# One norm's sums taken by TensorE, layer 0's set-up put behind the first feed-forward, and half a product put between two products on the same PSUM banks

## The chip, the cores and the metric

One core of a Trainium2 chip runs the whole program. The metric is the device time of one execution in microseconds (us); the time before is the median of three executions. Engines are named as in the profile: PE (TensorE), DVE (VectorE), ACT (ScalarE), POOL (GpSimd), SP (SyncE), and a "q" behind a name means its queue of DMA issues. All data are fp32.

## What is computed

Two decoder layers over 512 tokens of width 1024. Each layer is a feed-forward at half weight, a mixer, and a second feed-forward at half weight. The mixer of layer 0 is a hybrid (Mamba-2 heads beside mLSTM heads), that of layer 1 is sparse attention with a top-k choice of keys. Every one of the six stages starts from an RMS norm.

```python
def rms_norm(x, g):
    xf = x.astype(jnp.float32)
    y = xf * lax.rsqrt(jnp.mean(xf * xf, axis=-1, keepdims=True) + EPS) * g.astype(jnp.float32)
    return y.astype(x.dtype)

def swiglu(h, w_gate, w_up, w_down):          # D_MODEL 1024, D_FF 2816
    return (jax.nn.silu(h @ w_gate) * (h @ w_up)) @ w_down
...
x = x + 0.5 * swiglu(rms_norm(x, ffn_norm[l, 0]), ...)
x = x + mixer(rms_norm(x, mix_norm[l]), ...)
x = x + 0.5 * swiglu(rms_norm(x, ffn_norm[l, 1]), ...)
```

## The kernel before

**Stages and layout.** The stages run in the order ffn00, mix0, ffn01, ffn10, mix1, ffn11. The state x lies transposed in SBUF, as eight tiles of 128 features by 512 tokens (k = 0 to 7). An fp32 product is made as three matmuls of split operands, high by high, high by low and low by high (`mm3`, L263 to L265), so each operand exists as a pair of forms: ACT rounds the high part (L436) and DVE subtracts it to get the low part (L438).

**A feed-forward.** The 2816 hidden features are 11 units of 256 columns in three groups of 4, 4 and 3 units (`GROUPS`). When a group's hidden tiles are there, `down` multiplies them by the group's rows of the down-projection, for n = 0 and n = 1 (512 output features each). `down` calls `seven`, a product of two by two blocks in seven products instead of eight. The products accumulate in pairs of PSUM banks: A (tile `pA`), and D or B (tiles `pD` and `pB`, of one tag). A product is two halves (s = 0, 1), each of 12 matmuls of 256 columns in a group of four units and 9 in the group of three. Between products that go on in the same banks, what stands there is taken out first: `keep` copies it to SBUF on ACT (L581), and `c11`, `c22`, `c12` and `c21` add it to what was kept on DVE (L431 `ft<-pA,ft`) and then to x (L779). With n = 0 (`late=True`) the order of the seven products is A(A11), B(A12), D(S1), A(S2), A(S3), D(S4), A(A22); the two halves of A's S2 are kept by two ACT copies of 256 columns, after which S3 starts on the same banks. With n = 1 the order is A, D, A, B, A, D, A. There are 12 calls with n = 0: three groups in each of four feed-forwards.

**Forms of the weights.** `block` loads a piece of weights over SP's queue into one of 4 raw buffers, and `made` writes its forms into one of 5 form buffers. For S4 and A12 the form is "summed": ACT writes the negated high part (L463), a DMA on POOL's queue adds the raw weights onto it (L464), and ACT writes the high part (L465).

**What sets the order.** In the feed-forwards the steps are recorded in a `Plan` with a cost in us each; a list scheduler orders them and they are issued in that order on every engine, PE's in the order of the code. ffn00 is one plan, ffn01 with ffn10 the second, ffn11 the third. The code of the mixers and of the set-up is put in order by the framework's own scheduler. Each engine executes its instructions in order.

**The norm between stages.** As the last call of `down` finishes x, `prep_later` runs for each pair of tiles (dp = 0, 1 after n = 0, and 2, 3 after n = 1): ACT writes x times gain (L719), DVE its low part (L722), ACT the square (L732), and POOL adds the squares of k = 1 to 7 one after another onto `ssq` (L431 `ssq<-ssq,sq`, seven adds). `settle` then sums over the features with four matmuls by a column of ones (`pssq`, 8 records on PE, L694 in a plan, L378 otherwise); the last product of n = 1, `c21`, finishes x for dp = 2. The next stage's matmuls on x times gain begin before that; the factor from the norm goes in later (`prow`, then `rrow`). The first stage loads x and makes its norm in `load_x` (`prep`, L348, L366, L367). After the last stage, `store_later` transposes x on PE (`pot`, L803), copies it on ACT (L812) and stores it.

**Layer 0's set-up.** `setup_hybrid` loads four small parameter arrays over ACT's queue (`prow`, L290) and transposes them on PE (`ptpar`, L292); they are first used in mix0. It is called ahead of all stages.

Of the kernel before, what the change touches and what calls it, by code (L numbers as in the profile page):

```python
# [16 lines left out]
P = 128  # L17
# [62 lines left out]
class Plan:  # L80
# [9 lines left out]
    def __init__(self, tc):  # L90
        self.tc, self.steps, self.writer, self.readers, self.last, self.users = tc, [], {}, {}, {}, {}

# [76 lines left out]
    def issue(self):  # L169
        start = self.order()  # L170
        nc = self.tc.nc
        for i in sorted(range(len(start)), key=lambda i: (start[i], i)):
# [3 lines left out]
            for ins in nc.cur_bb.bb.instructions[n:]:  # L176
# [6 lines left out]
                self.last[ins.engine] = ins.name  # L183
        self.__init__(self.tc)
# [19 lines left out]
class Trunk:  # L204
# [146 lines left out]
    def prep(self, which, k):  # L351
# [16 lines left out]
        if k == KC - 2:  # L368
            self.xg, self.pending = [Feat(t) for t in self.xgn], 2
            self.xgk = lambda k: [("xg", which, i, k) for i in range(2)]  # L370

    def rms_col(self, ssq, n):
# [4 lines left out]
        for b in range(NB):  # L377
            nc.tensor.matmul(ps[:, b : b + 1], ssq[:, b * P : (b + 1) * P], self.ones1, start=True, stop=True)  # L378
# [14 lines left out]
    def settle(self):  # L393
# [3 lines left out]
        if self.pending == 2:  # L397
            self.rcol = self.rms_col(self.ssq(), D)
# [157 lines left out]
    def seven(self, raws, xf, late, kept, evac):  # L556
# [10 lines left out]
        def mul(ps, block, form, start, summed=False):  # L567
            j, f = self.made(block, summed)
            ps, psk = ps
            for s in range(2):  # L570
                col = slice(s * P, (s + 1) * P)
                for q in range(nq):
# [3 lines left out]
                    )  # L576

        def keep(to, ps, halves):
            (to, tok), (ps, psk) = to, ps
            for h in ((0, 1), (1, 2)) if halves else ((0, 2),):  # L580
                self.s((h[1] - h[0]) * H, lambda h=h: nc.scalar.activation(  # L581
                    to()[:, h[0] : h[1]], ps()[:, h[0] : h[1], 0:H], AF.Copy), [(*psk, s) for s in range(*h)], tok[h[0] : h[1]])
# [9 lines left out]
        keep(kept[0], A, False)  # L592
        if late:
# [4 lines left out]
            keep(kept[2], D, False)  # L598
            mul(A, less(t2, b22, b11), self.S2, False)
            keep(kept[1], A, True)  # L600
            mul(A, less(b12, b22, b12), self.S3, False)
            c22(A, kept[2])
            mul(D, b22, self.S4, False, True)
            c12(D, kept[1])
        else:
            mul(D, less(b11, b12, b11), self.S1, True)
            keep(kept[2], D, False)
            mul(A, less(t2, b22, b11), self.S2, False)
            keep(kept[1], A, False)
# [73 lines left out]
    def settle_later(self):  # L683

        nc = self.nc
        if self.pending == 2:
# [3 lines left out]
            ssq = self.ssq  # L690

            def sums():
                for b in range(NB):
                    nc.tensor.matmul(ps()[:, b : b + 1], ssq()[:, b * P : (b + 1) * P], self.ones1, start=True, stop=True)  # L694

            self.t(0.6, sums, ["ssq"], ["pssq"])
# [10 lines left out]
    def prep_later(self, which, k):  # L707
# [26 lines left out]
        if k == KC - 2:  # L734
# [893 lines left out]
```

## Time and profile before

| | us |
|---|---|
| median of three executions | 2085.14 (2084.42 to 2085.89) |
| the profiled execution | 2082.31 |
| its span in the trace | 2080.6 |
| PE busy in the span | 2021.5 (97%) |
| DVE busy | 1615.7 (78%) |
| ACT busy | 1148.6 (55%) |

A row of a timeline is: start in us, duration in us, engine, line, operation, output<-input, array and tile sizes, count, and in brackets the idle time of that engine just before it with what ended that idle time. Matmuls are pipelined: one of 256 columns is shown some 0.28 us long, while the next one starts some 0.12 us after it, so costs on PE are read from start to start. Some matmul records can be missing.

### The profile page before, as it was taken

How to read it: one execution, taken by the hardware profiler on the slowest of the kernel's cores; microseconds unless marked ns; L12 is line 12 of the kernel's file. 1: busy time of each engine (PE TensorE's matmuls, PEld its weight loads, DVE VectorE, ACT ScalarE, POOL GpSimd, SP SyncE). 2: the span in 40 equal slices, each digit the busy share in tenths (PEclk: the TensorE clock that was granted, in tenths of full speed). 3: DMA queues.
4: the chain of work that ended last, by engine and by line, in shares of the span. 5: the costliest groups of instructions: out<-in, count | busy, mean ns of one | idle time of the engine just before them, and what ended most of it. 6: DMA issues, size and time to landing. Idle time of an engine off the chain costs nothing.

```text
span 2080.6 us, 34030 instructions
## 1 busy us (share of the span) xinstructions
PE 2021.5 (97%) x13726; PEld 1812.4 (87%) x13726; DVE 1615.7 (78%) x2363; ACT 1148.6 (55%) x1678; POOL 282.0 (14%) x328
## 2 busy tenths in 40 slices
PE   6999999999999999999998999999997999999998
PEld 5999999887788888999998999999864468999998
DVE  5988878786537638989787988878789736988886
ACT  4666656442335435656565666657455624656564
POOL 2000001420001020000002000001215311001000
PEclk8999999999999999999999999999996999999999
DMA  4456565422221222665664456565420012556564
GB/s 134 122 156 170 149 166 131 130 87 71 71 82 61 81 92 81 153 173 149 156 150 114 122 157 169 150 165 134 130 67 11 1 41 71 142 153 165 150 165 110
DMA packets 203174, 248.65 MB, mean 120 GB/s; under 512 B 13452, under 2 KB 181512, under 8 KB 203016
## 3 DMA queue, kind: packets, MB, share of 16 engines
q1 hardware_dynamic: 184720, 185.52, 28.6%
q0 software_dynamic: 17280, 60.83, 15.8%
q8 instruction: 108, 1.77, 0.3%
q14 instruction: 50, 0.41, 0.1%
q10 hardware_dynamic: 1016, 0.13, 0.0%
HBM read 183.53 MB, written 2.10 MB: 89 GB/s over the span
## 4 chain that ended last, share of the span: by engine, by line
PE 92%; DVE 3%; DMA 1%; ACT 1%; issue 1%; POOL 0%; SPq 0%; ACTq 0%; DVEq 0%; POOLq 0%
PE pA L263 10%; PE pA L264 10%; PE pA L265 10%; PE pD L263 5%; PE pD L265 5%; PE pD L264 5%; PE pB L263 3%; PE pB L264 3%; PE pB L265 3%; PE ptok L263 3%; PE ptok L265 3%; PE ptok L264 2%; PE po L265 2%; PE po L263 2%; PE po L264 2%; PE po L1515 2%
## 5 line engine op out<-in xcount | busy, mean ns | idle before, releaser
L438 DVE TENSOR_TENSOR form<-raw,form 128x1024 fp32r<-128x1024 f32 (+1 forms) x332 | 395.7, 1200 | 120.4 <-ACT form L436 119.7
L436 ACT ACTIVATE form<-raw 128x1024 fp32r<-128x1024 f32 (+1 forms) x332 | 339.5, 1027 | 144.0 <-DVE raw L431 100.6
L263 PE MATMUL pA<-xf,form 128*128 128x256 f32 x1152 | 322.4, 280 | 0.0
L264 PE MATMUL pA<-xf,form 128*128 128x256 f32 x1152 | 322.4, 280 | 0.0
L265 PE MATMUL pA<-xf,form 128*128 128x256 f32 x1152 | 321.9, 279 | 0.0
L431 DVE TENSOR_TENSOR raw<-raw 128x1024 f32<-128x1024 f32 (+1 forms) x240 | 283.4, 1185 | 7.6 <-DMA raw<-in_ffn_w_up 3.4
L464 POOL DMA_DIRECT2D form<-raw x120 | 103.4, 861 | 1181.2 <-ACT form L463 1127.0
L263 PEld LDWEIGHTS pA<-xf,form 128*128 128x128 f32 x1152 | 216.8, 188 | 0.1
L264 PEld LDWEIGHTS pA<-xf,form 128*128 128x128 f32 x1152 | 216.3, 188 | 0.2
L265 PEld LDWEIGHTS pA<-xf,form 128*128 128x128 f32 x1152 | 216.4, 188 | 0.0
L263 PE MATMUL pA<-hid,form 128*128 128x256 f32 x704 | 201.0, 286 | 12.0 <-ACT ft L581 11.3
L463 ACT ACTIVATE form<-raw 128x1024 fp32r<-128x1024 f32 (+1 forms) x120 | 123.4, 1028 | 157.5 <-PE pD L265 133.7
L264 PE MATMUL pA<-hid,form 128*128 128x256 f32 x704 | 198.2, 282 | 0.8 <-DVE hid L438 0.8
L265 PE MATMUL pA<-hid,form 128*128 128x256 f32 x704 | 197.5, 281 | 0.0
L265 PE MATMUL pD<-xf,form 128*128 128x256 f32 x576 | 161.5, 280 | 0.0
L264 PE MATMUL pD<-xf,form 128*128 128x256 f32 x576 | 161.3, 280 | 0.0
L263 PE MATMUL pD<-xf,form 128*128 128x256 f32 x576 | 161.3, 280 | 0.0
L232 DVE TENSOR_TENSOR form<-raw,form 128x1024 fp32r<-128x1024 f32 (+2 forms) x85 | 102.3, 1204 | 64.1 <-ACT form L229 61.5
L431 DVE TENSOR_TENSOR ft<-ft 128x256 f32<-128x256 f32 (+2 forms) x288 | 146.9, 540 | 4.1
L229 ACT ACTIVATE form<-raw 128x1024 fp32r<-128x1024 f32 (+2 forms) x85 | 87.0, 1023 | 113.8 <-PE ptok L265 44.2
L263 PEld LDWEIGHTS pA<-hid,form 128*128 128x128 f32 x704 | 132.5, 188 | 17.5 <-ACT ft L581 16.5
L264 PEld LDWEIGHTS pA<-hid,form 128*128 128x128 f32 x704 | 132.4, 188 | 1.8 <-DVE hid L438 1.6
(372 smaller groups left out, 5298.2 us busy)
## 6 DMA issues: line engine op xcount, KB each, us to landing
form<-raw POOLq DMA_DIRECT2D x104, 512.0 KB, 5.6
raw<-in_ffn_w_gate SPq DMA_DIRECT2D x88, 512.0 KB, 4.4
raw<-in_ffn_w_up SPq DMA_DIRECT2D x88, 512.0 KB, 4.1
raw<-in_ffn_w_down SPq DMA_DIRECT2D x64, 512.0 KB, 4.8
raw<-in_hy_w_in SPq DMA_DIRECT2D x44, 512.0 KB, 3.5
raw<-in_ffn_w_down SPq DMA_DIRECT2D x32, 384.0 KB, 3.5
raw<-in_hy_w_out SPq DMA_DIRECT2D x16, 512.0 KB, 3.3
form<-raw POOLq DMA_DIRECT2D x16, 384.0 KB, 4.4
```

The source lines that it names most:

```text
L229: nc.scalar.activation(hi, src, AF.Copy)
L232: nc.vector.tensor_tensor(lo, src, hi.bitcast(F32), op=ALU.subtract)
L263: mm(out, l[0], r[0], start=start, stop=False)
L264: mm(out, l[0], r[1], start=False, stop=False)
L265: mm(out, l[1], r[0], start=False, stop=stop)
L431: (self.p if pool else self.v)(n, lambda: e.tensor_tensor(out(), x(), y(), op=op), reads, writes)
L436: self.s(n, lambda: nc.scalar.activation(hi(), src(), AF.Copy), srck, hik)
L438: n, lambda: nc.vector.tensor_tensor(lo(), src(), hi().bitcast(F32), op=ALU.subtract), srck + hik, lok
L463: self.s(n * w, lambda: nc.scalar.activation(f[:, 1], raw, AF.Copy, scale=-1.0), rawk, lok)
L464: self.plan.add("gpsimd", 0.85, lambda: nc.gpsimd.dma_start(f[:, 1], raw, accum_op=ALU.add), rawk + lok, lok, 5.5)
L1515: nc.tensor.matmul(po[par * 64 : par * 64 + 64], pr[s // 2][:, s % 2, V : V + 64], pT[par], start=(s == 0), stop=(s == b),)
```

## The change

Five edits:
1. In `seven` with `late=True`, A's S2 is kept by one ACT copy of 512 columns, and between S2 and S3 stands the first half (s = 0) of D's S4. Its second half stands where the whole of S4 stood, behind S3. S4's form is made before S3's.
2. In the last call of `down`, the pairs of tiles for n = 1 are prepared (or stored) in the order dp = 3, 2.
3. In `prep_later` the squares of the last pair (dp = 2) are no longer added by POOL. `pssq` takes them as two more operands: twelve matmuls (24 records) in place of four (8), and five POOL adds in place of seven. This is so in the three places where a feed-forward's `prep_later` feeds a norm: from ffn00 to mix0, from ffn01 to ffn10 and from ffn10 to mix1.
4. `setup_hybrid` is called at the start of mix0, behind the last PE instruction of ffn00's plan.
5. `rms_col` and the plan's `sums` share one function.

```diff
-        def mul(ps, block, form, start, summed=False):
-            j, f = self.made(block, summed)
+        def mul(ps, block, form, start, summed=False, f=None, ss=(0, 1)):
+            j, f = made = f or self.made(block, summed)
...
-            for s in range(2):
+            for s in ss:
...
-            keep(kept[1], A, True)
+            keep(kept[1], A)
+            f22 = mul(D, b22, self.S4, False, True, ss=(0,))
             mul(A, less(b12, b22, b12), self.S3, False)
             c22(A, kept[2])
-            mul(D, b22, self.S4, False, True)
+            mul(D, b22, self.S4, False, f=f22, ss=(1,))
             c12(D, kept[1])
...
+    def sums(self, ps, parts):
+
+        for b in range(NB):
+            for i, x in enumerate(parts):
+                self.nc.tensor.matmul(
+                    ps[:, b : b + 1], x[:, b * P : (b + 1) * P], self.ones1, start=i == 0, stop=i == len(parts) - 1
+                )
...
-            self.t(0.6, sums, ["ssq"], ["pssq"])
+            self.t(0.2 + 0.45 * len(ssqs), lambda: self.sums(ps(), [x() for x in ssqs]), self.ssqk, ["pssq"])
...
+            if last:
+                self.ssqs, self.ssqk = self.ssqs + [sq], self.ssqk + sk
+            elif j:
+                ssq = self.ssqs[0]
                 self.vtt(T, ssq, ssq, sq, ALU.add, ["ssq"], ["ssq"] + sk, True)
...
-                for dp in (2 * n, 2 * n + 1):
+                for dp in ((0, 1), (3, 2))[n]:
                     if nxt is None:
                         self.store_later(dp)
                     else:
-                        self.prep_later(nxt, 2 * dp)
+                        self.prep_later(nxt, 2 * dp, dp == 2)
...
-            self.setup_hybrid()
...
                 elif s == "mix0":
+                    with tc.issue_after(self.plan.tail[mybir.EngineType.PE]):
+                        self.setup_hybrid()
                     self.hybrid(nxt)
```

Lines of the change stand one to nine further down: `mm3` is L264 to L266, `keep` L590, the summed form L472 to L474, high parts L445.

**The order on PE in the first call with n = 0.** In the kernel before, these rows stand where S2 ends and S3 begins; a tile's number tells one tile from another of its name.

```order
L265 MATMUL pA_958<-hid_858,form_80 128x256
L263 MATMUL pA_958<-hid_962,form_80 128x256
L264 MATMUL pA_958<-hid_971,form_80 128x256
L265 MATMUL pA_958<-hid_962,form_80 128x256
L263 MATMUL pA_958<-hid_398,form_80 128x256
L264 MATMUL pA_958<-hid_429,form_80 128x256
```

S3's first matmul follows S2's last on the same tile. In the change, the same place reads as follows.

```order
L264 MATMUL pA_948<-hid_952,form_80 128x256
L265 MATMUL pA_948<-hid_961,form_80 128x256
L266 MATMUL pA_948<-hid_952,form_80 128x256
L264 MATMUL pD_1020<-hid_388,form_80 128x256
L265 MATMUL pD_1020<-hid_419,form_80 128x256
L266 MATMUL pD_1020<-hid_388,form_80 128x256
```

Twelve matmuls on pD (three of them shown) now stand between pA's S2 and pA's S3, and twelve fewer stand behind S3.

**The order on ACT ahead of the same place.** In the kernel before, L463 and L465 make S4's summed form and L581 are the keeps.

```order
L643 ACTIVATE ft_782<-pA_736 128x2x256
L436 ACTIVATE hid_962<-ft_782 128x256
L436 ACTIVATE hid_962<-ft_782 128x512
L463 ACTIVATE form_80<-raw_79 128x1024
L436 ACTIVATE hid_858<-ft_567 128x512
L465 ACTIVATE form_80<-raw_79 128x1024
L581 ACTIVATE ft_1047<-pA_958 128x512
```

In the change, L472 and L474 are the summed form and L590 the keep.

```order
L652 ACTIVATE ft_772<-pA_726 128x2x256
L472 ACTIVATE form_80<-raw_79 128x1024
L474 ACTIVATE form_80<-raw_79 128x1024
L445 ACTIVATE hid_952<-ft_772 128x256
L445 ACTIVATE hid_952<-ft_772 128x512
L445 ACTIVATE hid_848<-ft_557 128x512
L590 ACTIVATE ft_1024<-pA_948 128x512
```

The summed form moved ahead of two (its last part: three) instructions that make hidden forms.

**The order on PE at the start of mix0 in the change.** `pgate` are three of mix0's first products, `ptpar` is the set-up's transpose, `pssq` the norm's sums.

```order
L265 MATMUL pgate<-xgn,form 24x512
L266 MATMUL pgate<-xgn,form 24x512
L293 MATMUL ptpar<-raw,prow 128x76
L264 MATMUL pgate<-xgn,form 24x512
L265 MATMUL pgate<-xgn,form 24x512
L266 MATMUL pgate<-xgn,form 24x512
L378 MATMUL pssq<-raw,ssq 128x1
L378 MATMUL pssq<-raw,sq 128x1 x2
```

`ptpar` stood in ffn00's first unit, directly ahead of its `pssq`, and now stands here, 54 matmuls behind the last product of ffn00; three such pairs of `pssq` rows follow the one shown.

## Rows read from the trace of the kernel before

**Rows 1.** The head of the page: span, busy times, and the chain that ended last by engine.

```profile
span 2080.6 us, 34030 instructions
PE 2021.5 (97%) x13726; PEld 1812.4 (87%) x13726; DVE 1615.7 (78%) x2363; ACT 1148.6 (55%) x1678; POOL 282.0 (14%) x328
PE 92%; DVE 3%; DMA 1%; ACT 1%; issue 1%; POOL 0%; SPq 0%; ACTq 0%; DVEq 0%; POOLq 0%
```

**Rows 2.** The waits of PE over the span: us in total, times, longest.

```profile
PE pA L263 <- ACT ft L581: 11.3, 24, 0.5
PE ptpar L292 <- DMA prow<-in_hy_conv_w: 10.4, 1, 10.4
...
PE pssq L694 <- POOL ssq L431: 4.9, 1, 4.9
...
PE ptok L265 <- DVE xgn L722: 2.0, 2, 1.2
...
PE prow L390 <- POOL raw L382: 0.9, 1, 0.9
...
PE pot L803 <- DVE raw L779: 0.7, 2, 0.3
```

**Rows 3.** The timeline of PE where S2 ends and S3 runs, in ffn00's first call with n = 0.

```profile
125.98 0.28 PE L265 MATMUL pA<-hid,form 128*128 128x256 f32 x1
126.74 0.39 PE L263 MATMUL pA<-hid,form 128*128 128x256 f32 x1 [0.47 <-ACT ft L581]
126.96 0.28 PE L264 MATMUL pA<-hid,form 128*128 128x256 f32 x1
...
128.15 0.28 PE L265 MATMUL pA<-hid,form 128*128 128x256 f32 x1
128.90 0.39 PE L263 MATMUL pA<-hid,form 128*128 128x256 f32 x1 [0.47 <-ACT ft L581]
```

**Rows 4.** The timeline of ACT at the same place.

```profile
126.30 0.38 ACT L581 ACTIVATE ft<-pA 128x256 f32<-128x256 f32 x1 [1.16 <-PE pA L265]
...
128.46 0.38 ACT L581 ACTIVATE ft<-pA 128x256 f32<-128x256 f32 x1 [0.83 <-PE pA L265]
```

**Rows 5.** From the views of single lines: durations in ns (least, median, longest) of the instructions that empty pA, and for L464, the DMA that makes the summed form, the time to landing in us.

```profile
L581 ACT ACTIVATE ft<-pA x132: 383/597/603, 80.6 to 2065.1; 128x512 f32<-128x512 f32 x108, 128x256 f32<-128x256 f32 x24
L431 DVE TENSOR_TENSOR ft<-pA,ft x60: 677/692/694, 90.2 to 2069.5; 128x512 f32<-128x512 f32 x60
...
DMA to landing us min/median/max: 3.9/5.5/8.7
```

**Rows 6.** The timeline of POOL: the issue of S4's summed form ahead of the place of rows 3, and the one ahead of the third group's place, where PE's first wait ended at 345.67.

```profile
119.99 0.85 POOL L464 DMA_DIRECT2D form<-raw  x1 [10.12 <-ACT form L463]
...
340.95 0.86 POOL L464 DMA_DIRECT2D form<-raw  x1 [11.05 <-DVE form L438]
```

**Rows 7.** The start of ffn00: PE, then ACT, POOL and the chain of waits (start, us, what).

```profile
21.87 0.40 PE L265 MATMUL pg<-xgn,form 128*128 128x512 f32 x1
32.70 0.36 PE L292 MATMUL ptpar<-raw,prow 76*128 76x76 f32 x1 [10.44 <-DMA prow<-in_hy_conv_w]
32.86 1.81 PE L694 MATMUL pssq<-raw,ssq 128*128 128x1 f32 x8
...
28.06 1.06 ACT L436 ACTIVATE form<-raw 128x1024 fp32r<-128x1024 f32 x1 [6.08 <-DMA raw<-in_ffn_w_gate]
...
30.39 1.26 POOL L367 TENSOR_TENSOR ssq<-ssq,sq 128x512 f32<-128x512 f32 x1 [6.18 <-ACT sq L366]
...
28.07 4.39 DMA prow<-in_hy_conv_w
```

**Rows 8.** From ffn01 to ffn10: PE, then ACT, POOL and DVE.

```profile
1119.36 0.40 PE L265 MATMUL pg<-xgn,form 128*128 128x512 f32 x1
1124.68 1.87 PE L694 MATMUL pssq<-raw,ssq 128*128 128x1 f32 x8 [4.92 <-POOL ssq L431]
1126.41 0.77 PE L263 MATMUL pu<-xgn,form 128*128 128x512 f32 x1
...
1119.89 1.13 ACT L732 ACTIVATE sq<-raw 128x512 f32<-128x512 f32 x2
...
1117.44 7.19 POOL L431 TENSOR_TENSOR ssq<-ssq,sq 128x512 f32<-128x512 f32 x4 [7.32 <-ACT sq L732]
...
1114.31 1.22 DVE L438 TENSOR_TENSOR form<-raw,form 128x1024 fp32r<-128x1024 f32 x1
...
1117.84 2.33 DVE L438 TENSOR_TENSOR form<-raw,form 128x1024 fp32r<-128x1024 f32 x1
1120.09 5.75 DVE L722 SCALAR_TENSOR_TENSOR xgn<-raw,xgn 128x512 fp32r<-128x512 f32 x4
```

**Rows 9.** Windows: for each stretch its length and the busy time (count) of PE, PEld, DVE, ACT and POOL, the granted clock of PE, the share of the DMA engines and GB/s.

```profile
1125.00:1131.00 6.00, 6.00 (x19) 5.04 (x19) 2.05 (x4) 0.00 (x0) 1.03 (x1) 0.50 0.27 87
1470.00:1490.00 20.00, 17.34 (x108) 16.76 (x109) 12.72 (x23) 7.99 (x22) 7.90 (x9) 1.00 0.36 106
1557.00:1600.00 43.00, 29.18 (x100) 18.04 (x99) 42.19 (x124) 21.54 (x56) 28.26 (x24) 0.67 0.04 13
```

**Rows 10.** From ffn00 to mix0: PE's sums, and ACT's last square.

```profile
384.78 0.95 PE L378 MATMUL pssq<-raw,ssq 128*128 128x1 f32 x8
...
379.44 0.61 ACT L732 ACTIVATE sq<-raw 128x512 f32<-128x512 f32 x1
```

More of the change, by code (lines that the diff above doesn't have):

```diff
@@ L182, in issue @@
                     )
-                self.last[ins.engine] = ins.name
-        self.__init__(self.tc)
+                self.last[ins.engine], self.tail[ins.engine] = ins.name, ins
+        self.__init__(self.tc, self.tail)
 class Lazy:
@@ L376, in rms_col @@
         ps = self.aux("pssq", (T,))
-        for b in range(NB):
-            nc.tensor.matmul(ps[:, b : b + 1], ssq[:, b * P : (b + 1) * P], self.ones1, start=True, stop=True)
+        self.sums(ps, ssq)
         ms, rcol = (self.cols[:, self.turn, i] for i in range(2))
@@ L576, in mul, with keep @@
                     )
-        def keep(to, ps, halves):
+            return made
+        def keep(to, ps):
             (to, tok), (ps, psk) = to, ps
-            for h in ((0, 1), (1, 2)) if halves else ((0, 2),):
-                self.s((h[1] - h[0]) * H, lambda h=h: nc.scalar.activation(
-                    to()[:, h[0] : h[1]], ps()[:, h[0] : h[1], 0:H], AF.Copy), [(*psk, s) for s in range(*h)], tok[h[0] : h[1]])
+            self.s(T, lambda: nc.scalar.activation(to(), ps()[:, :, 0:H], AF.Copy), [(*psk, 0), (*psk, 1)], tok)
         def less(o, x, y):
@@ L591, in seven @@
         mul(A, b11, self.A11, True)
-        keep(kept[0], A, False)
+        keep(kept[0], A)
         if late:
@@ L606, in seven @@
             mul(D, less(b11, b12, b11), self.S1, True)
-            keep(kept[2], D, False)
+            keep(kept[2], D)
             mul(A, less(t2, b22, b11), self.S2, False)
-            keep(kept[1], A, False)
+            keep(kept[1], A)
             B = self.pair("pB", "pB")
@@ L689, in settle_later @@
             self.turn, self.rcol = 1 - self.turn, rcol
[L690 to L694, printed above, removed]
-            self.t(0.6, sums, ["ssq"], ["pssq"])
+            ssqs = self.ssqs
+            self.t(0.2 + 0.45 * len(ssqs), lambda: self.sums(ps(), [x() for x in ssqs]), self.ssqk, ["pssq"])
             self.v(4, lambda: nc.vector.tensor_scalar(ms, ps()[:, 0:NB], 1.0 / D, EPS, op0=ALU.mult, op1=ALU.add),
@@ L705, in settle_later, with prep_later @@
         self.pending = max(self.pending - 1, 0)
-    def prep_later(self, which, k):
+    def prep_later(self, which, k, last):
         nc = self.nc
@@ L973, in gate @@
                     yield
-            rc = self.rms_col(ssq, 512)
+            rc = self.rms_col([ssq], 512)
             yield
```

21 lines of the change are left out of this document (11 added, 10 removed).

## The prediction

> **What bounds the kernel now.** I read the head of the page first [rows 1]: PE is busy 97% of the span, and 92% of the chain that ended last is PE. So the change can gain only what PE idles, what PE runs at the lower clock, and PE instructions that go. The waits of PE come next [rows 2]: the two longest entries are 24 waits of 0.5 us on the keep of `pA` (11.3 us) and one of 10.4 us on the set-up's parameters; one of 4.9 us on POOL's sum of squares stands lower. These are the three that the change touches. Then I read each place in the timelines [rows 3, 4, 7, 8, 10]. The sum below is made against the profiled execution: span 2080.6 us, 1.7 us around it, 2082.3 in all. The median of the three timed executions, 2085.1, is 2.8 above it, and I carry the difference over to that.
>
> **Half a product between products.** In before, S2's last matmul starts at 125.98, the keep at 126.30, S3's first matmul at 126.74 and its second at 126.96 [rows 3, 4]. Unhindered, matmuls of 256 columns start 0.12 apart (126.96 to 128.15 in ten steps). So two steps take 0.98 instead of 0.24: one wait costs 0.74, not the 0.47 shown as idle, since the first matmul behind it is slow as well. There are 24 of them [rows 2], two in each of 12 calls: 24 x 0.74 = 17.8 us.
>
> In the change a half of S4 on pD stands in this place. Is it long enough? In the groups of four units it is 12 matmuls, so S3 starts 13 steps after S2's last start, at 1.55 us; in the group of three 9 matmuls, 10 steps, 1.19. The keep needs 0.28 (the last matmul), 0.04 to ACT's start, 0.60 for 512 columns [rows 5], 0.06 back to PE: 0.98. That leaves 0.57 and 0.21. The second half of S4 now covers c22, which is DVE's and takes 0.69 [rows 5]: with the same ends 1.07, leaving 0.48 and 0.12. Both fit if the engine is free. ACT was: it idled 1.16 and 0.83 until PE ended, just before the keeps [rows 4]. For DVE no row shows it, since in before a whole product covered c22. I take all 17.8; the lower bound is nothing (first rival), and more than this isn't there. One keep less per call saves ACT some 0.1, hidden.
>
> **Start.** PE idles from 22.3 to 32.70 for the parameters, then runs `pssq` [rows 7]. Without `ptpar` it waits for the last add on POOL, 30.39 + 1.26 = 31.65. That chain starts from the first weights, which free ACT at 28.06, and none of it moves. So `pssq` starts at 31.7 instead of 32.86: 1.2 gained. Most of the stall stays, and so does the lower clock behind it. Bounds: 0.5 to 1.5.
>
> **ffn01 to ffn10.** Here PE idles 4.92 until POOL has added the last square at 1124.63, though ACT had that square at 1121.02 [rows 8]; then the clock stands at 0.50 for 1125 to 1131 with PE busy throughout [rows 9], work that takes half of those 6 us at full clock. So the stall and its clock cost 4.9 + 3.0 = 7.9. In the change `pssq` waits for ACT's last squares and for the fifth add. `c21` now feeds the last pair, whose two products with the gain and two squares follow on ACT, and five adds end two adds earlier. The adds took 1.8 each beside DVE against 1.26 alone [rows 7, 8], so the fifth ends some 3.6 before 1124.63, at 1121.0, when the squares are ready too. What is left of the wait would be 1121.0 - 1119.8 = 1.3 if nothing else moved; the new order puts ACT's squares ahead of the products with the gain, so I take 0.7, with 0 and 3 as ends. With 0.7 the clock stays: between 1470 and 1490 PE idled 2.7 us in three pieces and kept 1.00 [rows 9]. At full clock eight `pssq` records take 0.95 [rows 10], of which the last one's own length is some 0.17, so 0.11 a record; 16 more cost 1.8. Net: -7.9 + 0.7 + 1.8 = -5.4.
>
> A row shows DVE's form at 1.22 without POOL's adds beside it and 2.33 with them [rows 8]. The Trainium skill, page "SBUF — State Buffer", section "Who interferes with whom", has a rule that fits: a DVE instruction with two SBUF inputs and a GpSimd instruction that reads SBUF share one read port, and the later one is fully blocked until the other ends. The trace agrees in that both get slower. By this rule two adds fewer would give DVE back some 2.2 us in this stretch, and the 0.7 would go to 0; the sum doesn't count on it.
>
> **ffn00 to mix0.** In before no wait shows here; `pssq` runs at 384.78 among full work. The 16 records cost 1.8. `ptpar` costs its 0.2 here. Its four DMAs are issued behind ACT's last squares. These ended at 380.05 in before [rows 10]; the landing took 4.39 after the first issue [rows 7], so 384.4, and `ptpar` stands three matmuls ahead of `pssq`, at about 384. I take no wait; bounds 0 to 3. Net +2.0.
>
> **ffn10 to mix1.** PE waits 2.0 for DVE's products with the gain and 0.9 for `prow` [rows 2]. The change spreads the sums among mix1's first products and puts 21 of these ahead of `prow`, so the 0.9 goes; 1.8 is added; with two adds fewer beside DVE I take half of the 2.0 as gone. Net -0.1, bounds -2 to +2. Behind this the scheduler also reorders DVE's top-k work; DVE is busy 42.2 of 43 us there and PE 29.2 [rows 9], and nothing of that work is added or removed: 0, between -4 and +4.
>
> **Tail.** With dp = 3 stored first, only the last pair's transposes wait for `c21`: of 0.7 of waits [rows 2] I take 0.4.
>
> **The sum.** -1.2 - 17.8 - 5.4 + 2.0 - 0.1 - 0.4 = -22.9. The profiled execution would take 2059.4, the median 2062.2, so 2062.
>
> **Rivals.**
> - *The banks come free late.* With DVE busy 78% [rows 1], `c22` may find it in a form of 1.22, and the keep may find ACT in one of 1.06 [rows 7, 8]. Per call the worst is 1.22 + 1.06 less the spare 0.12 + 0.21 in the 4 calls of three units (1.95) and 0.48 + 0.57 in the other 8 (1.2): 4 x 1.95 + 8 x 1.2 = 17.4, all of the gain. Against it: ACT's idle time ahead of the keeps [rows 4]. Half of it gives 2071.
> - *The sums still wait.* DVE's products with the gain ran to 1125.84 [rows 8], behind POOL's adds. If PE still idles 3 us at ffn10, the clock falls as before: 2.3 + 3.0 lost, with up to 3 at `ptpar`, together 7: 2069.
> - *Slower: S4's summed form comes late.* It is now needed when S2 ends, a product and its waits earlier, and its path runs over ACT, a DMA on POOL's queue and the landing. In before the issue at 119.99 and a median landing of 5.5 [rows 5, 6] give 125.5, 1.2 ahead of 126.74; in the group of three 340.95 + 3.9 (the shortest, for its smaller piece) gives 344.9, 0.8 ahead of 345.67. The gain of 22.9 is eaten at 1.9 a call in 12 calls, so it decides at a landing of some 8.5 us everywhere if the issue stays; the longest seen is 8.7. At 9.5 it is 12 x 2.8 = 33.6 against the 22.9: 2096. Against it: ACT now makes the form's first part two hidden forms earlier.
> - *The change doesn't do what it says.* The 0.74 waits also gave DVE and ACT time to make the next forms. If these bound instead, the stall moves from the keep to `form` or `hid`, and the 17.8 stays: 2080. Against it: no wait of PE for a form shows in [rows 2], and ACT idles at the keeps [rows 4].
>
> On the slower rival's transfer the traces have their row, 5.5 us [rows 5]. The Trainium skill, page "DMA: Bandwidth & Descriptors", section "Anatomy of one DMA — SWDGE (gpsimd) path", gives for such a transfer a fixed 2.0 us and its bytes at 436 GB/s; for 512 KB that would be an estimate of 3.2, by which the rival falls away. The trace's number is longer, and decides.
>
> **Chances.** Forecast 0.70 (its own range 2057 to 2067), banks late 0.11, sums still waiting 0.10, stall moved 0.05, slower 0.04. The range for 8 in 10 reaches from 2055 (two transitions at their better ends, mix1 4 better) to 2072 (either of the first two rivals). About 0.2%, 4.2 us, is what a measurement of this kernel tells from no change. The first three cases are all faster by more; of the stall that moved (-5, near the bound) 0.01 counts as faster and 0.04 as the same: faster 0.92, same 0.04, slower 0.04.
>
> **What would show it.** Right: the row of 24 waits of `pA` on ACT `ft` is gone and no wait on DVE `ft<-pA,ft` takes its place; `ptpar` waits nowhere near ten us; ahead of ffn00's `pssq` PE still idles some 9 us, now for POOL; PE's clock at 1125 to 1131, shifted, is 1.00, and `pssq` has 24 records of 2.7 us in three places. Wrong: waits of PE in each call on `form`, `hid` or DVE `ft`; a clock at 0.50 at the start of ffn10; a wait of `ptpar` in mix0; or a stretch of attention longer by more than 4 us.

## The result, and the profile after

The changed kernel takes 2074.68 us (median of six executions, 2067.87 to 2082.13) against 2085.67 (six, 2084.42 to 2089.04) for the kernel before. The ratio is 0.9946 [0.9923, 0.9969]: faster, by 11 us instead of the 22.9 forecast, and above the range that ended at 2072. The profiled execution took 2076.09; its pair is the 2082.31 from which the sum started.

The head of the page of after, with the chain that ended last by engine, answers to [rows 1].

```profile
span 2074.3 us, 34103 instructions
PE 2029.2 (98%) x13774; PEld 1818.2 (88%) x13774; DVE 1614.9 (78%) x2363; ACT 1147.1 (55%) x1666; POOL 273.4 (13%) x322
...
PE 88%; DVE 5%; DMA 4%; issue 2%; ACT 1%; POOL 0%; SPq 0%; ACTq 0%; POOLq 0%; DVEq 0%
```

PE's busy time has risen by 7.7 us though its waits got fewer: 48 more records, and time at the lower clock, which counts as busy. PE's share of the last chain fell from 92% to 88%, DVE's rose from 3% to 5%. The waits of PE in after answer to [rows 2].

```profile
PE pssq L378 <- POOL ssq L368: 10.2, 1, 10.2
PE pqk L1487 <- DVE st L1492: 6.1, 4, 3.2
...
PE pg L265 <- DVE xgn L726: 1.7, 2, 1.0
PE pA L265 <- DVE hid L447: 1.5, 5, 0.7
...
PE ptok L265 <- DVE form L233: 1.0, 1, 1.0
PE pot L810 <- DVE raw L786: 0.7, 1, 0.7
...
PE pA L264 <- ACT hid L445: 0.6, 1, 0.6
```

The 24 waits on the keep are gone, and no wait for `c22`'s `ft` or for S4's form took their place. The waits of `pA` for hidden forms are 2.1 in all (1.5 on DVE, 0.6 on ACT) where before had 0.8; none of them stands between S2 and S4. `ptpar` waits nowhere. The wait of 4.9 for POOL's sum at ffn10 is gone; two for DVE's `xgn`, 1.7 together, are new. The place of [rows 3], on PE:

```profile
124.78 0.28 PE L266 MATMUL pA<-hid,form 128*128 128x256 f32 x1
124.90 0.28 PE L264 MATMUL pD<-hid,form 128*128 128x256 f32 x1
...
126.20 0.28 PE L266 MATMUL pD<-hid,form 128*128 128x256 f32 x1
126.32 0.28 PE L264 MATMUL pA<-hid,form 128*128 128x256 f32 x1
126.44 0.29 PE L265 MATMUL pA<-hid,form 128*128 128x256 f32 x1
```

And the keep on ACT, which answers to [rows 4]:

```profile
125.10 0.60 ACT L590 ACTIVATE ft<-pA 128x512 f32<-128x512 f32 x1 [0.77 <-PE pA L266]
```

From S2's last start to S3's first are 13 steps of 0.12, 1.54 us. The keep ends at 125.70, 0.62 before S3; the prediction had 1.55 and 0.57. This part came out as worked out.

Where, then, are the other 12 us? The program is cut at attention: from the first transpose of a query on PE (`pqt`, the start of mix1's score work) to the last mixer's end (`prow` of ffn11). The columns of the two views that follow are those of [rows 9]: length, busy times, clock, DMA share, GB/s. First the kernel before:

```profile
1561.51:1743.75 182.24, 170.97 (x649) 102.12 (x649) 118.56 (x310) 85.91 (x196) 64.48 (x80) 0.89 0.09 27
```

Then after:

```profile
1548.52:1741.07 192.55, 179.56 (x648) 104.75 (x649) 120.86 (x308) 86.04 (x196) 65.33 (x80) 0.83 0.08 25
```

The same work takes 10.3 us more, at a granted clock of 0.83 instead of 0.89. Time at the lower of the two levels is 2 x (1 - clock) x length: 40 us before, 65 after (to 2 us, as the clock has two digits). All the rest of the span went from 1898.4 (2080.6 - 182.24) to 1881.8, 16.6 less. By stretch, from the starts of the same PE instructions in both traces:

| stretch | forecast | measured |
|---|---|---|
| start, to ffn00's `prow` | -1.2 | -0.7 |
| ffn00 and mix0 | -2.4 | -2.5 |
| ffn01, to ffn10's `prow` | -9.8 | -7.3 |
| ffn10, to the first `pqt` | -4.5 | -2.5 |
| attention | 0 | +10.3 |
| ffn11 and the tail | -4.8 | -3.6 |

Two questions stand: what each edit gave, and whether attention's 10 us belong to the change.

### The profile page after: what moved, and what is told of

It is laid out like the page before. It is cut to its first block, busy times and chain, and to the rows that moved or that the text cites. A ratio compares the mean times of both kernels' runs of the same rounds, so it can differ in the third digit from the quotient of the medians.

```text
span 2074.3 us, 34103 instructions
## 1 busy us (share of the span) xinstructions
PE 2029.2 (98%) x13774; PEld 1818.2 (88%) x13774; DVE 1614.9 (78%) x2363; ACT 1147.1 (55%) x1666; POOL 273.4 (13%) x322
## 3 DMA queue, kind: packets, MB, share of 16 engines
q8 instruction: 108, 1.77, 0.3%
## 4 chain that ended last, share of the span: by engine, by line
PE 88%; DVE 5%; DMA 4%; issue 2%; ACT 1%; POOL 0%; SPq 0%; ACTq 0%; POOLq 0%; DVEq 0%
PE pA L265 9%; PE pA L264 9%; PE pA L266 9%; PE pD L266 5%; PE pD L265 5%; PE pD L264 5%; PE ptok L266 3%; PE ptok L264 2%; PE ptok L265 2%; PE pB L265 2%; PE pB L264 2%; PE pB L266 2%; PE po L266 2%; PE po L264 2%; PE po L265 2%
## 5 line engine op out<-in xcount | busy, mean ns | idle before, releaser
L445 ACT ACTIVATE form<-raw 128x1024 fp32r<-128x1024 f32 (+1 forms) x332 | 340.0, 1028 | 164.9 <-DVE raw L440 118.3
L264 PE MATMUL pA<-xf,form 128*128 128x256 f32 x1152 | 321.8, 279 | 0.0
L266 PE MATMUL pA<-xf,form 128*128 128x256 f32 x1152 | 321.5, 279 | 0.0
L473 POOL DMA_DIRECT2D form<-raw x120 | 103.6, 863 | 1161.8 <-ACT form L472 1087.3
L264 PEld LDWEIGHTS pA<-xf,form 128*128 128x128 f32 x1152 | 216.5, 188 | 0.1
L266 PEld LDWEIGHTS pA<-xf,form 128*128 128x128 f32 x1152 | 216.3, 188 | 0.0
L472 ACT ACTIVATE form<-raw 128x1024 fp32r<-128x1024 f32 (+1 forms) x120 | 123.5, 1029 | 137.9 <-PE pD L266 77.5
L264 PE MATMUL pA<-hid,form 128*128 128x256 f32 x704 | 198.0, 281 | 0.7 <-ACT hid L445 0.6
L266 PE MATMUL pA<-hid,form 128*128 128x256 f32 x704 | 197.2, 280 | 0.0
L266 PE MATMUL pD<-xf,form 128*128 128x256 f32 x576 | 161.3, 280 | 0.0
L264 PE MATMUL pD<-xf,form 128*128 128x256 f32 x576 | 160.9, 279 | 0.0
L264 PEld LDWEIGHTS pA<-hid,form 128*128 128x128 f32 x704 | 132.4, 188 | 1.2 <-ACT hid L445 0.8
```

Of the source, the lines that this page charges most:

```text
L264: mm(out, l[0], r[0], start=start, stop=False)
L266: mm(out, l[1], r[0], start=False, stop=stop)
L445: self.s(n, lambda: nc.scalar.activation(hi(), src(), AF.Copy), srck, hik)
L472: self.s(n * w, lambda: nc.scalar.activation(f[:, 1], raw, AF.Copy, scale=-1.0), rawk, lok)
L473: self.plan.add("gpsimd", 0.85, lambda: nc.gpsimd.dma_start(f[:, 1], raw, accum_op=ALU.add), rawk + lok, lok, 5.5)
```

## The experiments

Kernels timed on the same chip shared the executions of the kernel before. "Low" is attention's time at the lower clock, "rest" the span less attention. All these come from one profiled execution of each run; the medians and ratios come from all of them.

| kernel | median, us | ratio to before | attention | low | rest |
|---|---|---|---|---|---|
| *first chip: before 2090.99, 22 executions* | | | | | |
| half product alone | 2071.55 | 0.9915 [0.9892, 0.9939] | 198.70 | 79 | 1883.5 |
| sums alone | 2087.94 | 0.9988 [0.9965, 1.0011] | 192.37 | 69 | 1900.1 |
| set-up alone | 2090.64 | 1.0002 [0.9987, 1.0017] | 189.65 | 53 | 1899.8 |
| the change | 2072.92 | 0.9915 [0.9883, 0.9948] | 184.65 | 41 | 1882.6 |
| *second chip: before 2087.18, 13 executions* | | | | | |
| before again | 2092.04, one | | 186.88 | 49 | 1903.4 |
| half product, set-up | 2067.01 | 0.9899 [0.9866, 0.9932] | 179.50 | 36 | 1882.4 |
| inner sums repeated | 2087.16, one | | 180.25 | 36 | 1905.2 |
| change with fillers | 2072.86 | 0.9934 [0.9912, 0.9956] | 186.98 | 22 | 1884.2 |
| *third chip: before 2090.01, 11 executions* | | | | | |
| the change | 2073.08 | 0.9918 [0.9891, 0.9944] | 190.23 | 61 | 1885.7 |
| half product, set-up | 2069.11 | 0.9903 [0.9889, 0.9916] | 182.81 | 44 | 1884.7 |
| half product, set-up, order | 2066.23 | 0.989 [0.9876, 0.9904] | 179.42 | 36 | 1883.3 |
| half product, set-up, fillers | 2076.69 | 0.9945 [0.993, 0.9961] | 192.73 | 46 | 1879.9 |

**The parts alone.** The starting theory was that the half product gave what it should and the loss lay behind the sums and in attention; the rival, that the half product itself gave about half.

Edit 1 alone, as in the diff of the change (`keep` of 512 columns, S4's first half ahead of S3):

```diff
+            f22 = mul(D, b22, self.S4, False, True, ss=(0,))
             mul(A, less(b12, b22, b12), self.S3, False)
...
-            mul(D, b22, self.S4, False, True)
+            mul(D, b22, self.S4, False, f=f22, ss=(1,))
```

> The kernel before with edit 1 alone (the half product between S2 and S3, one keep). Theory A (the half product does what the sum said): the 24 waits of pA on ACT ft go, the stretches of the four feed-forwards shorten by 12 x 1.48 = 17.8 us together, and outside attention nothing else changes. Theory B (the order of attention decides): the scheduler puts DVE's and ACT's work of attention in another order here too, so the stretch from mix1's prow to the end-of-mixer pssq (256.8 us in before, 266.3 in the change) differs from 256.8 by several us. A alone gives 2067 to 2068; A with an attention as long as the change's gives 2077.

Edits 2, 3 and 5 alone:

```diff
-                        self.prep_later(nxt, 2 * dp)
+                        self.prep_later(nxt, 2 * dp, dp == 2)
...
-            self.t(0.6, sums, ["ssq"], ["pssq"])
+            self.t(0.2 + 0.45 * len(ssqs), lambda: self.sums(ps(), [x() for x in ssqs]), self.ssqk, ["pssq"])
```

> The kernel before with edits 2, 3 and 5 alone (last squares summed by pssq, tiles in the order 3, 2). Theory C (one-column matmuls cost the clock): behind each of the three rows of 24 one-column matmuls the granted clock falls to 0.50 for some 3 us, though PE never idles there; per place 1.8 for the records and 1.5 to 1.7 for the clock, so mix0 starts 3.3 later than without, and ffn10 gains 5.3 + 3.3 - 3.3 = 5 at most. Rival (the clock fell in the change for another reason, the set-up's transpose or the denser work before): the clock stays at 1.00 at mix0. Time by C with attention as in before: 2085.4 - 5 + 3.3 + 2 = 2085 to 2086.

Edit 4 alone:

```diff
-            self.setup_hybrid()
...
+                    with tc.issue_after(self.plan.tail[mybir.EngineType.PE]):
+                        self.setup_hybrid()
```

> The kernel before with edit 4 alone (set-up behind ffn00). Predicted for the start: pssq 1.2 earlier, and 0.2 for the transpose in mix0, no wait for its DMA: 2084.4. If the order of attention decides (theory B), that stretch differs from 256.8 us here too, although nothing of this edit lies within 1000 us of it, and the total moves by the same amount.

The change itself beside them:

> The change once more, for a second trace. If its times vary by 14 us because attention runs at a clock that differs between executions, the two traces agree within 0.3 us in every stretch outside mix1 and differ in mix1 alone, with another granted clock there (0.60 and 0.77 for 1550 to 1600 and 1600 to 1650 in the first trace). If the variation comes from DMA or the feed-forwards, they differ elsewhere.

Measured: the half product alone takes 0.9915, and so does the whole change; neither other part differs from before. The column "rest" says it without attention's noise. The three kernels of the table without the half product and with nothing added (sums alone, set-up alone, before again) stand at 1899.8 to 1903.4, the first trace of before at 1898.4. All kernels with it stand at 1879.9 to 1885.7, whatever else they hold. So the half product gives 13 to 24 us between single traces, 17 by the middles. The twelve places themselves say it more exactly. From the start of S2's first matmul to that of S4's last one on PE they take 110.1 to 110.2 us together in each of the five traces without the half product, and 92.3 to 92.6 in each of the nine with it. That is 17.6 to 17.9 less, against 17.8 forecast. The other edits add nothing to it that shows.

On this chip and the third one the change gained 18 and 17 us by the medians, against 11 in the first comparison. There all six executions of before lay in 2084.42 to 2089.04, while the 46 taken later reach from 2083.24 to 2099.16. Part of the shortfall is thus the baseline, whether by chance or by the chip. And the one trace from which the forecast started (2082.31) was faster than every other execution of that kernel.

The half product alone has its worst attention in this table, 198.70, in an execution of 2083.93; five of its other six took 2069.7 to 2071.7. Its window row:

```profile
1550.71:1749.41 198.70, 187.53 (x648) 107.36 (x649) 118.24 (x310) 85.73 (x196) 64.56 (x80) 0.80 0.08 24
```

The same 648 matmuls as in after, DVE, ACT and POOL with the same busy times to 3 us, and a clock of 0.80.

**What the sums add beside the half product.** From `pA`'s last matmul of ffn01 to ffn10's `prow`, PE takes 20.3 us in before, 14.2 with the sums alone (-6.2, near the -5.4 forecast), 17.6 with the half product alone, and 17.7 in the change. So the sums gain there alone, but nothing once the half product is there. The four traces with the half product and the set-up but without the sums on PE take 16.0 to 16.3 there, and the change 17.7, 17.7 and 19.3 in its three: beside these two edits the sums cost time. PE's waits in that place with the half product alone:

```profile
PE pg L264 <- DVE xgn L722: 2.0, 2, 1.2
PE pssq L694 <- POOL ssq L431: 1.2, 1, 1.2
PE pA L263 <- DVE ft L431: 1.0, 1, 1.0
```

The wait of 4.9 has become 1.2 without any change of the sums. What is late next is DVE's low part of x times gain. In the change, PE, then POOL and DVE:

```profile
1110.41 0.50 PE L265 MATMUL pg<-xgn,form 128*128 128x512 f32 x1 [1.01 <-DVE xgn L726]
...
1112.10 0.50 PE L265 MATMUL pg<-xgn,form 128*128 128x512 f32 x1 [0.72 <-DVE xgn L726]
...
1114.05 0.28 PE L378 MATMUL pssq<-raw,ssq 128*128 128x1 f32 x2
...
1108.34 1.47 POOL L440 TENSOR_TENSOR ssq<-ssq,sq 128x512 f32<-128x512 f32 x1 [3.83 <-ACT sq L735]
...
1109.89 1.61 POOL L440 TENSOR_TENSOR ssq<-ssq,sq 128x512 f32<-128x512 f32 x1
...
1108.58 1.77 DVE L726 SCALAR_TENSOR_TENSOR xgn<-raw,xgn 128x512 fp32r<-128x512 f32 x1
...
1110.28 1.76 DVE L726 SCALAR_TENSOR_TENSOR xgn<-raw,xgn 128x512 fp32r<-128x512 f32 x1
```

`pssq` waits for nothing. PE waits 1.0 and 0.7 earlier, for low parts of 1.77 and 1.76 beside POOL's adds of 1.47 and 1.61. With no add beside it a low part takes 0.74 in this trace, and POOL's add in [rows 7] takes 1.26. Two adds went, but the ones that are left meet just the low parts that PE needs first. The low part that begins 0.24 behind its add and the one that begins 0.39 behind its own both end 0.55 behind that add's end (1109.81 to 1110.36 and 1111.49 to 1112.04). In the fourteen traces 136 low parts begin while POOL adds squares. The 124 that begin 0.01 to 1.33 behind the add's start all end 0.55 or 0.56 behind its end; the other 12, which begin 1.6 behind its start, when it is nearly through, end 0.70 or 0.71 behind it. So some 0.55 of the 0.74 is done only when the add is through, however early the low part began. By the Trainium skill, page "SBUF — State Buffer", section "Who interferes with whom", a DVE instruction with two SBUF inputs contends with a GpSimd instruction that reads SBUF for a port pair that is an exclusive lock; the trace agrees, with these 0.55 us.

**The half product with the set-up.** The change without its edits 2, 3 and 5, which the theory said were worth nothing:

```diff
-                for dp in ((0, 1), (3, 2))[n]:
+                for dp in (2 * n, 2 * n + 1):
...
-            self.t(0.2 + 0.45 * len(ssqs), lambda: self.sums(ps(), [x() for x in ssqs]), self.ssqk, ["pssq"])
+            self.t(0.6, sums, ["ssq"], ["pssq"])
```

> The change without edits 2 and 3: half product and set-up move alone, POOL adds all squares. If the two extra operands of pssq cost as much as they save (records and clock, theory C), everything outside attention takes what it takes in the change, 1882 us, within 2. If they save the 5.4 us that the prediction gave them at ffn10, it takes 1887 to 1889. Behind pssq the clock stays at 1.00 at mix0.

Before once more, for its spread:

> The kernel before once more, for a second trace. Theory D (attention's length follows the time that PE's clock stands at 0.50 there, and that differs between executions of any of these kernels): all stretches but attention agree with the first trace of before within 1 us, attention (first pqt to the last mixer's prow, 182.2 us in the first trace with 41 us at the lower clock) is longer by about 0.4 us for each us more at the lower clock. Theory B (the order of attention decides, and before has a good one): attention takes 182 us again.

On the third chip the change and this kernel side by side:

> The change, beside the next three on one chip. If edits 2 and 3 bring nothing beside the half product, it takes what the kernel without them takes, within 0.2% in the median; if the 24 one-column matmuls cost the clock in most executions, it is 2 to 5 us slower than that.

> Half product and set-up move alone, again, beside the change on one chip. By theory C with the new wait at ffn10 gone in both: 2 to 5 us faster than the change in the median. If its first times (2063.6 to 2068.9) were luck with attention's clock, both have the same median.

Measured: 2067.01 and 2069.11, 4 us less than the change on the chip that ran both, with intervals that touch (0.9903 [0.9889, 0.9916] against 0.9918 [0.9891, 0.9944]). Its eight executions lie in 2063.6 to 2069.2, the sixteen of the change in 2063.3 to 2082.8. "Rest" is the same; what differs is attention: 179.50 and 182.81 here against 192.55, 184.65 and 190.23.

The granted clock over the whole span is on record for each execution counted here, and it tells more than the few traces. In the change, the six of sixteen executions at 0.982 or more took 2063.3 to 2073.0 (median 2068.6), the ten below it 2072.2 to 2082.8 (median 2077.1). All eight of the kernel without edits 2, 3 and 5 stand at 0.982 or more, with a median of 2068.6. Before has 32 of 47 there, with a median of 2087.0. So at a like clock the change and this kernel take the same time, some 18 us less than before. What sets them apart is how often the clock is low; sixteen and eight executions, in part on different chips, suggest but don't prove that the change is worse in this.

**Attention and the clock.** In the kernels without fillers, attention's length goes with its time at the lower clock: from 179.5 us at 36 to 198.7 at 79, some 0.44 us for each. But it does so between executions of one and the same kernel too (184.65 at 41 and 192.55 at 65 for the change, 182.24 at 40 and 186.88 at 49 for before). To see whether the clock is the cause, filler matmuls were put where PE waits in attention; their results are overwritten before anyone reads them, so in what is computed they add nothing. Twelve of 512 columns in the change, four ahead of the first `pqt` and the others ahead of score matmuls:

```diff
+                    for _ in range(4 if b == 0 and h == 0 else 0):
+                        nc.tensor.matmul(pq.rearrange("p a t -> p (a t)"), self.ident, self.xT[:, 0], start=True, stop=True)
...
+                if b < 2 and i == 0:
+                    nc.tensor.matmul(ps[:, 0:T], self.ident, self.xT[:, 0], start=True, stop=True)
```

> The change with matmuls of 512 columns that nothing reads put where PE waits at the start of attention (four ahead of the first pqt, one ahead of each row of pqk for the first two blocks; some 12 x 0.85 us at full clock; the real results overwrite them). Theory D: the time at the lower clock falls from 41 to 64 us to under 25, and attention takes 170 to 178 us; the total is 2060 to 2066 and varies less. Theory B: attention is bound by DVE's chain, the clock makes no difference, and the matmuls only add: 190 to 200 us.

And nine in the half product with the set-up, four ahead of the first `pqt` and five behind it:

```diff
+                for _ in range(5 if b == 0 and g8 == 0 and par == 0 and i == 0 else 0):
+                    nc.tensor.matmul(ps[:, 0:T], self.ident, q[0][:, 0, 0:T], start=True, stop=True)
```

> Half product and set-up move, with nine matmuls that nothing reads in two waits of attention alone (four ahead of the first pqt, five between pqt and the first pqk, in waits of 3.8 and 3 to 5 us). Theory D: the time at the lower clock falls below 30 us, and since the matmuls lie in waits, attention takes 250 to 260 us (262 with 38 us at the lower clock): median 2055 to 2062. Rival (the first blocks of attention are bound by DVE's and ACT's chain, whatever the clock): 260 to 266 us, no gain in the median.

Measured: in the first, the clock rose to 0.94, the highest of all, and attention still took 186.98 us; the median, 2072.86, is the change's. Seven of its fillers lie inside the stretch, with 1.1 to 2.1 us each. In the second the clock did not rise (46 us low, against 36 and 44 without the fillers). It got slower by 7.6 us on its chip (2076.69 against 2069.11), and attention took 192.73, with 4.46 for the five fillers inside it. Its PE at the first transposes:

```profile
1548.48 1.09 PE L1458 MATMUL pqt<-raw,q 128*128 128x128 f32 x8 [0.26 <-DVE q L1342]
1560.39 1.94 PE L1458 MATMUL pqt<-raw,q 128*128 128x128 f32 x8 [5.44 <-DVE q L1342]
```

And in the same kernel without fillers:

```profile
1551.47 1.94 PE L1456 MATMUL pqt<-raw,q 128*128 128x128 f32 x8 [3.79 <-DVE q L1342]
...
1564.99 1.97 PE L1456 MATMUL pqt<-raw,q 128*128 128x128 f32 x8 [0.41 <-DVE q L1342]
```

The wait ahead of the first transposes, 3.8 without the fillers, is 0.3 with them, and the next transposes waited 5.4 for DVE instead of 0.4. But these stand elsewhere, behind 8 score matmuls and the fillers instead of 24 score matmuls. The scheduler put attention in another order in both kernels with fillers: outside the longest order that each has in common with the same kernel without them are 39 of 648 matmul records and 41 of 307 DVE instructions in the first, 51 of 648 and 73 of 309 in the second. So neither run changes the clock alone. Shown is that a clock of 0.94 did not come with a shorter attention: 182.24 at 0.89 in before and 179.50 in the half product with the set-up are below its 186.98. Whether the clock sets the length or the waits bring down the clock is not shown, and the link between the two is a correlation. What in an order of the instructions makes the clock fall more or less stays open.

**The sums and the clock.** Behind the sums at mix0 the clock of after falls while PE never idles:

```profile
376.00:380.00 4.00, 4.00 (x32) 3.57 (x30) 1.62 (x3) 1.06 (x1) 0.37 (x1) 1.00 0.45 133
380.00:381.00 1.00, 1.00 (x5) 0.75 (x4) 0.00 (x0) 0.00 (x0) 0.67 (x1) 0.68 0.88 247
381.00:383.00 2.00, 2.00 (x6) 1.63 (x5) 0.00 (x0) 0.00 (x0) 0.00 (x0) 0.50 0.39 136
383.00:384.00 1.00, 1.00 (x4) 0.78 (x4) 0.00 (x0) 0.00 (x0) 0.00 (x0) 0.61 0.00 0
384.00:390.00 6.00, 6.00 (x30) 4.93 (x29) 2.94 (x5) 1.65 (x2) 0.77 (x1) 1.00 0.08 19
```

The 24 records stand at 376.62 to 379.22; then come 2 x (0.32 + 2 x 0.50 + 0.39) = 3.4 us at the lower level, work that takes half of that at full clock, so some 1.7 lost. To test whether the one-column matmuls do it, the kernel before issued the sums of mix0's two inner norms three times over (each matmul starts its sum anew, so the outcome is the same), where no other part of the change stands:

```diff
-            nc.tensor.matmul(ps[:, b : b + 1], ssq[:, b * P : (b + 1) * P], self.ones1, start=True, stop=True)
+            for _ in range(reps):
+                nc.tensor.matmul(ps[:, b : b + 1], ssq[:, b * P : (b + 1) * P], self.ones1, start=True, stop=True)
...
-            rc = self.rms_col(ssq, 512)
+            rc = self.rms_col(ssq, 512, 3)
```

> The kernel before with the sums of mix0's two inner norms issued three times over (12 matmuls in place of 4, one column each, same result; nothing else). Theory C: behind each of the two the granted clock falls to 0.50 for some 3 us, and mix0's inner stretch (prow of the first to prow behind the second) is longer by 2 x (1.8 + 1.5) = 6.6 us. Rival (the clock fell at the transitions for what stands around pssq there): the clock stays at 1.00 and 2 x 1.8 = 3.6 us are added.

PE at the first of the two norms:

```profile
667.45 2.73 PE L379 MATMUL pssq<-raw,ssq 128*128 128x1 f32 x24
670.05 0.68 PE L1262 MATMUL pn<-v,e 128*128 128x257 f32 x2
```

And the windows behind the first and around the second:

```profile
668.00:670.00 2.00, 2.00 (x20) 2.00 (x19) 0.52 (x2) 0.00 (x0) 0.00 (x0) 1.00 0.46 162
671.00:674.00 3.00, 3.00 (x9) 2.35 (x8) 0.42 (x1) 1.30 (x7) 0.47 (x1) 0.50 0.00 0
704.00:712.00 8.00, 8.00 (x56) 7.24 (x55) 2.23 (x4) 2.34 (x4) 1.01 (x1) 1.00 0.18 60
```

24 records take 2.60 instead of 0.81 for eight, 1.8 more, as the prediction had it. Behind the first norm the clock fell with PE busy; behind the second it did not. From mix0's `prow` to ffn01's it took 402.59 instead of 396.74: 5.85 more, of which 2 x 1.8 is the records, so that some 2.2 is left for the one fall, with 0.65 between two traces of before (its second has 397.39). With the norm ahead of mix0 counted in, 24 records were followed by a fall in four of seven places (the change twice in three traces, the sums alone once, the change with fillers not, and here once in two). Eight records there were followed by one in none of nine traces, and at the two inner norms in none of 26 places. So the sums seem able to bring it on with PE never idle; a share of four in seven is no rule, and when they do is open.

At mix1's norm it shows too, though PE waits there (0.96 in after, among the records). Behind the 24 records the clock fell in four of five traces, in after by 2 x 0.43 x 4.00 = 3.4 us:

```profile
1462.00:1466.00 4.00, 4.00 (x18) 4.00 (x18) 1.55 (x6) 1.18 (x4) 1.03 (x1) 0.57 0.36 122
```

The four traces of kernels that have eight records there, without the half product (before twice, the set-up alone, the inner sums repeated), show waits of 1.2, 0.8 and 0.9 and no fall.

**The order and the set-up, without the sums on PE.** Edits 1, 2 and 4, with POOL adding all squares:

```diff
-        if k == KC - 2:
+        if k == 4:
...
-                for dp in (2 * n, 2 * n + 1):
+                for dp in ((0, 1), (3, 2))[n]:
```

> Half product, set-up move and edit 2 (tiles in the order 3, 2), with POOL adding all squares as in before: the change without the one-column matmuls. At ffn10 the last add comes later than the squares, so PE waits for POOL at pssq again, 2 to 4 us, with a fall of the clock behind it; the tail gains its 0.4. Total 2 to 4 us above the kernel without edit 2. If the order 3, 2 alone does good at ffn10, no such wait and equal times.

Measured: 2066.23 (2064.45 to 2068.33), 0.989 [0.9876, 0.9904]: faster than before by 24 us, and the lowest median of all, 7 us under the change on the same chip (their intervals touch). Though POOL adds all squares, no wait at ffn10's `pssq` appears in it, where 2 to 4 us had been expected. Its four executions stand at a clock of 0.985 or 0.986, so it is ahead of the others at a like clock by some 2 us (2066.2 against 2068.6), which four executions can't settle.

## Why the prediction was wrong

- **"Half a product between products", 17.8: right.** Steps of 0.12, spare 0.62 for ACT, no wait for `c22` or for S4's form, and the twelve places shorter by 17.6 to 17.9 in every trace that has it. The rival of banks that come free late and that of a stall moved to the forms both fall; so does the slower one: L473's landings are still 3.9, 5.5 and 8.7 (least, median, longest), and nothing waited.
- **"Start", 1.2: right in kind**: `pssq` starts at 31.55 instead of 32.86, and the stretch is 0.7 shorter in this pair; PE idles 10.2 ahead of `pssq`, now for POOL. The set-up alone shows nothing in the total.
- **"ffn01 to ffn10", -5.4: failed.** Measured is -2.6 (20.3 to 17.7). The 4.9 was taken as if it would stand with the half product in place; that alone cuts it to 1.2, so the edits don't add. And "With 0.7 the clock stays" is wrong in its ground: PE waited 1.7 ahead of the sums, nothing at them, and the clock still fell behind them:

```profile
1116.00:1118.00 2.00, 2.00 (x13) 1.81 (x13) 2.00 (x5) 0.00 (x0) 0.94 (x1) 0.91 0.89 289
1118.00:1120.00 2.00, 2.00 (x6) 1.53 (x5) 0.78 (x1) 0.00 (x0) 0.54 (x1) 0.50 0.30 103
1120.00:1122.00 2.00, 2.00 (x8) 1.53 (x8) 0.00 (x0) 0.00 (x0) 0.00 (x0) 0.74 0.80 254
1122.00:1124.00 2.00, 2.00 (x11) 1.62 (x10) 0.00 (x0) 0.00 (x0) 0.00 (x0) 1.00 0.00 0
```

  That is 2 x (0.18 + 1.00 + 0.52) = 3.4 us at the lower level, 1.7 lost. Whether the two waits or the 24 records brought it on can't be told in this trace. Elsewhere each came without the other: with two like waits (1.2 and 0.7) and eight records the half product with the set-up had a fall that began at 1113.2 in its first trace, ahead of its sums at 1115.92, and none in its second; with 24 records and a single wait of 1.0, eight us ahead of them, the sums alone had none. The rival "the sums still wait" had the nearest time, 2069, with the clock falling as it said; but the wait it rested on was not at the sums.
- **"ffn00 to mix0", +2.0: the terms right, one missing.** 1.8 for the records and `ptpar` without a wait; the fall behind them, some 1.7, is not in the sum. The stretch of ffn00 and mix0 still came out at -2.5 in this trace; in the trace of the change on the first chip it was larger than before's by 0.1. A shift of 2.5 between two executions is the size of the term, so this row can't confirm it.
- **"ffn10 to mix1", -0.1: within its bounds of 2, with the same term missing**: -2.5 for the stretch against -4.5. The second trace of the change, the one without a fall of the clock behind mix1's sums, had -4.6; the third, with a fall, -2.6.
- **"0, between -4 and +4" for attention: failed, the step that cost most.** +10.3 in this pair, +2.4 in the change's second trace, +8.0 in its third. It also took before's one trace, 182.24, for the kernel's typical attention; the next trace of before had 186.88. The bounds came from an argument that no work is added or removed. They should have come from the spread of the stretch itself, which one trace cannot show: 43 us in which PE runs at 0.67 [rows 9] were the hint that this stretch is not a fixed one.
- **"Tail", 0.4: right at the end, eaten ahead of it.** Before has two waits of 0.35 at the transposes. The one ahead of the last transposes is gone, and the end, counted from the end of the last `c21` on DVE, came 0.33 sooner (5.78 instead of 6.10). The one behind n = 0 grew to 0.68, as it did in the half product with the set-up (0.7 of 1.0 in two waits), so the waits together stay at 0.7.

Two of the prediction's own signs of being wrong came: a clock at 0.50 at the start of ffn10, and an attention longer by more than 4 us. The rival "the sums still wait" named the first of them.

The shortfall of 12 in the first comparison is thus: some 6 from the terms outside attention (16.6 instead of 22.9, of which the twelve places give 17.7, so that all the other terms came to +1.1 instead of -5.1), and attention, whose +10 in the profiled pair became less over the medians. How much of attention's part is the change's new order and how much the executions that happened to be compared isn't settled. That its median is 4 us above the half product's with the set-up, on the same chip and with the same "rest", and that its executions have a lower clock more often, speaks for a part that belongs to the order; it is not shown.

## What to carry to other kernels

A wait that recurs in a fixed pattern is a safe term: its gain is the start-to-start loss times the count, and here 17.6 to 17.9 of 17.8 came. Single waits near each other are not additive: before pricing one, ask whether another edit already removes it, and what stands next behind it. Where the program has a long stretch in which PE waits for other engines, with a granted clock well under 1, take two or three profiled executions for its spread before summing anything against one, and let the range carry that spread.

## What was not expected of the hardware

- Twenty-four matmul records of one column, with PE busy ahead, through and behind them, were followed by some 3 us at a granted clock of 0.50 in four of seven places (three times 24 in a row, once 20 in a row with four ahead of them).
- A low part on DVE (0.74 us by itself) that begins while POOL adds squares ends 0.55 us behind that add's end, whether it began 0.01 or 1.33 us behind the add's start.
- Attention in one and the same kernel took 184.65, 190.23 and 192.55 us in three executions, with 41, 61 and 65 us at the lower clock. With more matmuls on PE, in another order, the clock was 0.94 and attention not shorter.
- The change moves nothing in attention by its text, and so does the set-up's move a thousand microseconds earlier; yet in both the framework's scheduler issues attention's instructions in another order. Outside the longest order in common with before are 29 of 648 matmul records and 37 of 309 DVE instructions with the set-up alone, 67 and 74 in the change. The two traces of before have one and the same order there.
